# A masked softmax on one core: fewer control instructions on VectorE, and GpSimd's set-up inside its loop

## The chip, the core and the metric

The kernel runs on one core of a Trainium2 chip. The core has compute engines that run their own instruction streams and meet at semaphores: TensorE (PE), VectorE (DVE), ScalarE (ACT) and GpSimd (POOL); a fifth, SyncE (SP), issues DMAs. Sixteen DMA engines move data between HBM, the chip's main memory, and SBUF, the core's on-chip memory of 128 partitions. The metric is device time in microseconds (us) of one execution, the median of several runs.

## The reference

The input is `x`, float32 of 16 batches x 8 heads x 256 x 256, and `lengths`, 16 integers, one per batch, drawn from 128 to 255. For each batch the first `length` columns of each row get a softmax and the rest is zero:

```python
for b in range(batch):
    length = lengths[b]
    masked = x[b, :, :, :length].copy()
    masked = masked - np.max(masked, axis=-1, keepdims=True)
    exp_masked = np.exp(masked)
    result[b, :, :, :length] = exp_masked / np.sum(exp_masked, axis=-1, keepdims=True)
```

`x` and the result are 33.55 MB each. Columns beyond a batch's length need not be read.

## The kernel before

A batch is one tile of 128 partitions x 16 rows x 256 columns, 2.1 MB. Eight such tiles fit in SBUF (`xt`, 8 slots), and batch b uses slot b mod 8. A batch goes through five steps.

1. Load. SyncE issues the loads of batches 0 to 3 whole, at the start (L130, L132). GpSimd issues those of batches 4 to 15, two to a turn of a loop of six turns (L177). It reads the batch's length into a register (`length`, L120) and goes through a tree of branches (`pick`, L147) to one of twelve DMAs that differ in the width they load: 160 to 240 columns in steps of 8, or all 256. The tree stands twice in the program, for the even and the odd batch of a turn. From the second turn on, each load first waits until the load two batches before it has landed (`s_sw`) and until the store that frees its slot has landed (`s_st`).
2. Clip. VectorE takes the minimum of the tile and a value that is hugely negative beyond the length (`clip`, L218; L221): `down` is -1e30 x (column + 0.5), `len_s` is 1e30 x length. So no length is needed in an address. `mask` (L230) waits for the load and then clips columns 128 to 255, and, under a branch on the length (L238), columns 0 to 127 as well. With the lengths given, the branch is never entered.
3. Exponential. ScalarE runs over half tiles, 32 turns of a loop, with eight activations each that also sum their row (L326). No maximum is subtracted. A half turn i waits for `s_min` of i + 1; a whole clip adds 2, a half clip (batch 0) adds 1.
4. Divide. VectorE takes the reciprocal of eight row sums per partition (L245) and multiplies the half tile (L248).
5. Store. SyncE issues the stores of a batch in one to three parts (L141). Each waits for the divided half; a batch's first one waits also until the store two batches before has landed (L140). The very first store waits until ScalarE has done three halves (L134).

VectorE's order is written out by hand: the clip of the next batch comes after the first divided half of this one (batch 0 and batches 4 on) or ahead of it (batches 1 to 3).

Before its loop, GpSimd runs a set-up: the column numbers (`iota`, L164), constants for two small matmuls (L167, L168), two one-element memsets that stand in for stores that do not exist (L170), and, after VectorE has `len_s`, four memsets that fill columns 160 to 255 of slots 4 to 7 (L173), since a narrow load leaves them unwritten. It then waits for the lengths, the fills and batch 2's load (L176).

At the end a check looks whether any row sum is out of range (L274, L277; a matmul adds the flags over the partitions, L191). If so, all batches are done again with the maximum subtracted, in a slow loop at the end of VectorE's and ScalarE's programs (L293, L336). With the data given, it is not entered.

Of the kernel before, what the change touches and what calls it, by code (L numbers as in the profile page):

```python
# [9 lines left out]
F32 = mybir.dt.float32  # L10
# [11 lines left out]
def kernel(  # L22
# [6 lines left out]
    nc = tc.nc  # L29
# [13 lines left out]
    ahead = 4  # L43
    assert slots - ahead == 4 and batch % slots == 0

# [35 lines left out]
    ones_c = pool.tile([P, 1], BF16, name="ones_c")  # L81
    ends = pool.tile([P, 2], F32, name="ends")
    bad = pool.tile([P, 2], BF16, name="bad")
    count = psum.tile([1, 2], F32, name="count")
    redo = pool.tile([1, 1], F32, name="redo")
# [7 lines left out]
    with tc.tile_critical(no_gpsimd_drain=True):  # L93
# [53 lines left out]
        def pick(v, n, slot, par, ws):  # L147
# [15 lines left out]
        o_g = out_f.rearrange("b p t c -> p b (t c)")  # L163
        nc.gpsimd.iota(  # L164
            iota_i, pattern=[[1, seq_k]], base=0, channel_multiplier=0
        ).then_inc(s_iota, 1)
        nc.gpsimd.memset(ones, 1.0).then_inc(s_ones, 1)  # L167
        nc.gpsimd.memset(ones_c, 1.0).then_inc(s_ones, 1)  # L168
        for par in range(2):
            nc.gpsimd.memset(seed[:, par : par + 1], 0.0).then_inc(s_st[par], 64)  # L170
        nc.gpsimd.wait_ge(s_v, 2)
        for b in range(ahead, slots):
            nc.gpsimd.memset(xt[:, b, :, low:], 0.0).then_inc(s_fill, 1)  # L173
        nc.gpsimd.wait_ge(s_word, 16)
        nc.gpsimd.wait_ge(s_fill, slots - ahead)
        nc.gpsimd.wait_ge(s_ld[ahead - 1], 16)  # L176
        with nc.Fori(0, (batch - ahead) // 2, 1, engines=[POOL]) as q:  # L177
            for par in range(2):
                n = 2 * q + (ahead + par)
                v_len = length(POOL, word[0:1, bass.ds(2 * n, 1)])  # L180
                with nc.gpsimd.If(q >= 1):  # L181
                    nc.gpsimd.wait_ge(s_sw[par], 16 * q)
                    nc.gpsimd.wait_ge(s_st[par], 64 * q)
                pick(v_len, bass.ds(n, 1), bass.ds(n % slots, 1), par, widths + [seq_k])

# [3 lines left out]
        nc.tensor.matmul(len_f, lhsT=ones, rhs=len_b, start=True, stop=True).then_inc(s_lenf, 1)  # L189
        nc.tensor.wait_ge(s_bad, 2)  # L190
        nc.tensor.matmul(count, lhsT=ones_c, rhs=bad, start=True, stop=True).then_inc(s_count, 1)  # L191
# [4 lines left out]
        def step(ins):  # L196
            nonlocal v
            v += 1
            ins.then_inc(s_v, 1)
# [30 lines left out]
        def mask(b, s):  # L230
            v_len = length(DVE, word[0:1, 2 * b : 2 * b + 1])
            if b == 0:
                nc.vector.wait_ge(s_ld[s.start // half], 16)
            elif b < ahead:
                nc.vector.wait_ge(s_ld[b + 1], 16)
            else:
                nc.vector.wait_ge(s_sw[b % 2], 16 * ((b - ahead) // 2 + 1))
            with nc.vector.If(v_len < mid):  # L238
                clip(b, s, 0, mid)
            clip(b, s, mid, seq_k).then_inc(s_min, (s.stop - s.start) // half)  # L240

# [28 lines left out]


        sums = row_sum.rearrange("p b t -> p (b t)")
        for k, op in enumerate((ALU.max, ALU.min)):
            step(nc.vector.tensor_reduce(out=ends[:, k : k + 1], in_=sums, op=op, axis=AX))  # L274
        nc.vector.wait_ge(s_v, v)
        for k, (edge, op) in enumerate(((sum_high, ALU.is_gt), (sum_low, ALU.is_lt))):
            nc.vector.tensor_scalar(  # L277
                out=bad[:, k : k + 1],
                in0=ends[:, k : k + 1],
                scalar1=edge,  # L280
                scalar2=None,
                op0=op,
            ).then_inc(s_bad, 1)
# [8 lines left out]
        with nc.vector.Else():  # L292
            with nc.Fori(0, batch, 1, engines=[DVE]) as i:  # L293
# [12 lines left out]
                ).then_inc(g_v, 1)  # L306
                nc.vector.wait_ge(g_exp, i + 1)
                nc.vector.reciprocal(out=inv_g, in_=sum_g).then_inc(g_v, 1)
# [11 lines left out]
        sum_h = row_sum.rearrange("p b (h j) -> p (b h) j", h=2)  # L320
        with nc.Fori(0, 2 * batch, 1, engines=[ACT]) as i:
            nc.scalar.wait_ge(s_min, i + 1)
            at = bass.ds(i % (2 * slots), 1)
            for j in range(half):
                e = x_h[:, at, j, :]
                ins = nc.scalar.activation(  # L326
                    out=e, in_=e, func=EXP, accum_out=sum_h[:, bass.ds(i, 1), j]
                )
            ins.then_inc(s_exp, 1)

        nc.scalar.wait_ge(s_redo, 1)
        a_redo = length(ACT, redo_bits[0:1, 0:1])
        with nc.scalar.If(a_redo >= 1):
            for par in range(2):
                nc.scalar.wait_ge(s_st[par], 64 * (batch // 2 + 1))
            with nc.Fori(0, batch, 1, engines=[ACT]) as i:  # L336
                nc.scalar.dma_start(out=g_t, in_=x_g[:, bass.ds(i, 1)]).then_inc(g_ld, 16)
                nc.scalar.wait_ge(g_v, 3 * i + 2)
                for t in range(nt):
                    ins = nc.scalar.activation(  # L340
                        out=g_t[:, t],
                        in_=g_t[:, t],
                        func=EXP,
                        bias=neg_max[:, t : t + 1],
                        accum_out=sum_g[:, t : t + 1],
                    )
                ins.then_inc(g_exp, 1)
                nc.scalar.wait_ge(g_out, i + 1)
# [37 lines left out]
```

## Time and profile before

| what | us |
|---|---|
| median of 3 runs | 156.16 (155.8 to 156.35) |
| the profiled execution's own time | 156.34 |
| its span, first to last instruction of the kernel | 154.7 |
| DVE busy | 116.6 (75%) |
| ACT busy | 105.2 (68%) |
| POOL busy | 19.0 (12%) |
| last load landed | 134.2 |
| last store issued | 147.1 |

Times within the profile count from the span's start. Busy time of an engine leaves out its branches, register operations and waits. A queue's share is the time of its packets over sixteen DMA engines' span. A name such as DVEq is an engine's sequencer, which handles the instructions that are not counted as busy. In the chain of waits each step is followed back to what released it, and "issue" is time for which the trace shows no reason.

### The profile page before, as it was taken

The page shows a single profiled execution, that of the slowest core. Times are in us where ns is not written, and L with a number is a line of the kernel's source. Part 1 is how long each engine was busy: PE and PEld are TensorE (multiplying, and loading weights), DVE is VectorE, ACT ScalarE, POOL GpSimd, SP SyncE. Part 2 cuts the span into 40 slices and gives each one's busy share as a digit, 9 for nine tenths or more (in the row PEclk, how much of TensorE's full clock was granted, in tenths as well). Part 3 has the DMA queues.
Part 4 walks back from the last instruction along what each step waited for, and adds up shares of the span by engine and source line. Part 5 has one row for each costly group of instructions (what it writes and reads, how often), then busy time and mean ns, then how long its engine had stood idle before and what let it go on. Part 6 is the DMA issues. An engine that isn't in the chain of part 4 may idle for free.

```text
span 154.7 us, 1341 instructions
## 1 busy us (share of the span) xinstructions
PE 0.3 (0%) x2; PEld 0.2 (0%) x2; DVE 116.6 (75%) x89; ACT 105.2 (68%) x514; POOL 19.0 (12%) x26
## 2 busy tenths in 40 slices
PE   0000000000000000000000000000000000000000
PEld 0000000000000000000000000000000000000000
DVE  1349999953999696979879696969669619696820
ACT  3097799992692959688695959595964914959300
POOL 4910031000220200202020020202001000000000
DMA  3999999999999999999999999999999999999991
GB/s 114 430 447 419 441 373 420 403 407 447 406 403 391 410 410 417 412 416 412 404 422 409 415 412 409 421 414 412 415 424 415 416 437 432 422 447 424 424 426 76
DMA packets 9989, 62.09 MB, mean 401 GB/s; under 512 B 850, under 2 KB 946, under 8 KB 6274
## 3 DMA queue, kind: packets, MB, share of 16 engines
q1 hardware_dynamic: 5904, 41.95, 65.7%
q0 software_dynamic: 4080, 20.12, 32.1%
q14 instruction: 3, 0.02, 0.0%
q10 hardware_dynamic: 2, 0.00, 0.0%
HBM read 28.51 MB, written 33.55 MB: 401 GB/s over the span
## 4 chain that ended last, share of the span: by engine, by line
DMA 77%; issue 7%; DVE 4%; ACT 3%; POOLq 3%; SPq 1%; ACTq 0%; POOL 0%; PE 0%; DVEq 0%
DMA xt<-in_x_dram 77%; ACT xt L326 3%; DVE xt L221 2%; DVE xt L248 1%; POOLq L120 1%; POOLq L156 1%; POOLq L151 1%; SPq L130 1%; DVE ends L274 0%; ACTq L326 0%; POOL xt L151 0%; SPq L132 0%; POOLq L181 0%; DVE bad L277 0%; DVE inv_sum L245 0%
## 5 line engine op out<-in xcount | busy, mean ns | idle before, releaser
L326 ACT ACTIVATE xt<-xt x256 | 102.4, 402 | 37.7 <-DVE xt L221 37.7
L248 DVE TENSOR_TENSOR xt<-xt,inv_sum 128x2048 f32<-128x2048 f32 x32 | 73.3, 2291 | 1.1
L326 ACT ACTIVATION_READ_ACCUMULATOR xt<-xt x256 | 48.0, 188 | 0.0
L221 DVE SCALAR_TENSOR_TENSOR xt<-down,len_s,xt 128x2048 f32<-128x2048 f32 (+1 forms) x17 | 37.8, 2221 | 13.6 <-DMA xt<-in_x_dram 13.5
L151 POOL DMA_DIRECT2D xt<-in_x_dram x12 | 12.8, 1064 | 96.0 <-DMA out_dram<-xt 54.2
L245 DVE RECIPROCAL inv_sum<-row_sum 128x8 f32<-128x8 f32 x32 | 6.3, 198 | 14.4 <-ACT xt L326 14.4
L173 POOL MEMSET xt<- 128x1536 f32 x4 | 5.3, 1391 | 1.1 <-DVE len_s L212 1.1
L318 ACT ACT_TABLE_LOAD x1 | 1.3, 1283 | 1.6 <-SPq L93 1.6
L204 DVE TENSOR_SCALAR down<-iota_i 128x256 f32<-128x256 int32 x1 | 0.3, 301 | 1.6 <-POOL iota_i L164 1.6
L274 DVE TENSOR_REDUCE ends<-row_sum 128x1 f32<-128x256 f32 x2 | 0.7, 411 | 0.0
L191 PE MATMUL count<-bad,ones_c 128*1 128x2 bf16 x1 | 0.2, 164 | 145.3 <-DVE bad L277 145.3
L209 DVE CAST len_b<-word 1x16 bf16<-1x16 int32 x1 | 0.2, 164 | 0.4 <-DMA word<-in_lengths_dram 0.4
L212 DVE TENSOR_SCALAR len_s<-len_f 128x16 f32<-128x16 f32 x1 | 0.2, 173 | 0.3 <-PE len_f L189 0.3
L164 POOL IOTA iota_i<- 128x256 int32 x1 | 0.3, 331 | 0.6 <-SPq L93 0.6
L285 DVE TENSOR_REDUCE redo<-count 1x1 f32<-1x2 f32 x1 | 0.1, 148 | 0.3 <-PE count L191 0.3
L191 PEld LDWEIGHTS count<-bad,ones_c 128*1 128x1 bf16 x1 | 0.1, 79 | 145.4 <-DVE bad L277 145.4
L170 POOL MEMSET seed<- 1x1 f32 x2 | 0.2, 226 | 0.0
L277 DVE TENSOR_SCALAR bad<-ends 128x1 bf16<-128x1 f32 x2 | 0.2, 152 | 0.0
L318 ACT ACTIVATE warm<-const-float32-0.0 128x1 f32<-128x1 f32 x1 | 0.2, 204 | 0.0
L167 POOL MEMSET ones<- 1x128 bf16 x1 | 0.2, 196 | 0.0
L189 PE MATMUL len_f<-len_b,ones 1*128 1x16 bf16 x1 | 0.2, 165 | 2.6 <-DVE len_b L209 2.6
L370 POOL MEMSET const-float32-0.0<- 128x1 f32 x1 | 0.1, 98 | 0.3 <-issue 0.3
(6 smaller groups left out, 0.5 us busy)
## 6 DMA issues: line engine op xcount, KB each, us to landing
out_dram<-xt SPq DMA_DIRECT2D x19, 1024.0 KB
out_dram<-xt SPq DMA_DIRECT2D x14, 512.0 KB
xt<-in_x_dram SPq DMA_DIRECT2D x3, 2048.0 KB, 16.0
out_dram<-xt SPq DMA_DIRECT2D x3, 2048.0 KB
xt<-in_x_dram POOLq DMA_DIRECT2D x3, 1728.0 KB, 16.9
xt<-in_x_dram POOLq DMA_DIRECT2D x2, 2048.0 KB, 18.5
xt<-in_x_dram POOLq DMA_DIRECT2D x2, 1600.0 KB, 17.1
xt<-in_x_dram POOLq DMA_DIRECT2D x2, 1280.0 KB, 15.1
```

What stands on the lines that cost most here:

```text
L120: return nc.values_load(at, engines=[engine], skip_runtime_bounds_check_because="compared with constants, never an address",)
L130: nc.sync.dma_start(out=xt[:, 0, s], in_=x_f[0, :, s]).then_inc(s_ld[h], 16)
L151: nc.gpsimd.dma_start(out=xt[:, slot, :, :w], in_=x_n[:, n, :, :w]).then_inc(s_sw[par], 16)
L156: with nc.gpsimd.If(v <= ws[m]):
L173: nc.gpsimd.memset(xt[:, b, :, low:], 0.0).then_inc(s_fill, 1)
L191: nc.tensor.matmul(count, lhsT=ones_c, rhs=bad, start=True, stop=True).then_inc(s_count, 1)
L221: return nc.vector.scalar_tensor_tensor(out=t, in0=down[:, None, lo:hi].to_broadcast([P, s.stop - s.start, hi - lo]), scalar=len_s[:, b : ...
L245: step(nc.vector.reciprocal(out=inv_sum[:, b, s], in_=row_sum[:, b, s]))
L248: nc.vector.tensor_tensor(out=t, in0=t, in1=inv_sum[:, b, s, None].to_broadcast([P, half, seq_k]), op=ALU.mult,).then_inc(s_out, 1)
L274: step(nc.vector.tensor_reduce(out=ends[:, k : k + 1], in_=sums, op=op, axis=AX))
L318: nc.scalar.activation(out=warm, in_=nc.const_aps.tensor(0.0, (P, 1), F32), func=EXP)
L326: ins = nc.scalar.activation(out=e, in_=e, func=EXP, accum_out=sum_h[:, bass.ds(i, 1), j])
```

## The change

VectorE: `mask` no longer reads the length and no longer branches; it clips columns 128 to 255 alone. In place of the branch, the check at the end gets a third test, whether the smallest length is under 128; if it is, the slow loop redoes all batches. `s_min` now counts one per clip, so ScalarE's half turn i waits for i // 2 + 2. ScalarE's first half turn is written out before the loop, with constant addresses. In the slow loop, sixteen activations in a row become a loop.

GpSimd: the loop gets a turn more. Turn 0 goes to the `Else` of a branch, where the set-up now stands, behind the code of the loads; the turns from 1 on run the loads with q = (turn + 7) mod 8, which is turn - 1.

```diff
-    ends = pool.tile([P, 2], F32, name="ends")
-    bad = pool.tile([P, 2], BF16, name="bad")
-    count = psum.tile([1, 2], F32, name="count")
+    ends = pool.tile([P, 3], F32, name="ends")
+    bad = pool.tile([P, 3], BF16, name="bad")
+    count = psum.tile([1, 3], F32, name="count")
...
-        nc.gpsimd.iota(
-            iota_i, pattern=[[1, seq_k]], base=0, channel_multiplier=0
-        ).then_inc(s_iota, 1)
...
-        with nc.Fori(0, (batch - ahead) // 2, 1, engines=[POOL]) as q:
-            for par in range(2):
-                n = 2 * q + (ahead + par)
-                v_len = length(POOL, word[0:1, bass.ds(2 * n, 1)])
-                with nc.gpsimd.If(q >= 1):
-                    nc.gpsimd.wait_ge(s_sw[par], 16 * q)
-                    nc.gpsimd.wait_ge(s_st[par], 64 * q)
-                pick(v_len, bass.ds(n, 1), bass.ds(n % slots, 1), par, widths + [seq_k])
+        turns = (batch - ahead) // 2
+        with nc.Fori(0, turns + 1, 1, engines=[POOL]) as turn:
+            with nc.gpsimd.If(turn >= 1):
+                q = nc.s_assert_within(
+                    (turn + 7) % 8, 0, turns - 1, skip_runtime_bounds_check_because="turn >= 1"
+                )
+                for par in range(2):
+                    n = 2 * q + (ahead + par)
+                    v_len = length(POOL, word[0:1, bass.ds(2 * n, 1)])
+                    with nc.gpsimd.If(turn >= 2):
+                        nc.gpsimd.wait_ge(s_sw[par], 16 * q)
+                        nc.gpsimd.wait_ge(s_st[par], 64 * q)
+                    pick(v_len, bass.ds(n, 1), bass.ds(n % slots, 1), par, widths + [seq_k])
+            with nc.gpsimd.Else():
+                nc.gpsimd.iota(
+                    iota_i, pattern=[[1, seq_k]], base=0, channel_multiplier=0
+                ).then_inc(s_iota, 1)
...
+                nc.gpsimd.wait_ge(s_ld[ahead - 1], 16)
...
-        nc.tensor.wait_ge(s_bad, 2)
+        nc.tensor.wait_ge(s_bad, 3)
...
         def mask(b, s):
-            v_len = length(DVE, word[0:1, 2 * b : 2 * b + 1])
...
-            with nc.vector.If(v_len < mid):
-                clip(b, s, 0, mid)
-            clip(b, s, mid, seq_k).then_inc(s_min, (s.stop - s.start) // half)
+            clip(b, s, mid, seq_k).then_inc(s_min, 1)
...
-        for k, op in enumerate((ALU.max, ALU.min)):
-            step(nc.vector.tensor_reduce(out=ends[:, k : k + 1], in_=sums, op=op, axis=AX))
+        checks = (
+            (sums, ALU.max, sum_high, ALU.is_gt),
+            (sums, ALU.min, sum_low, ALU.is_lt),
+            (len_s, ALU.min, mid * big, ALU.is_lt),
+        )
+        for k, (values, op, _, _) in enumerate(checks):
+            step(nc.vector.tensor_reduce(out=ends[:, k : k + 1], in_=values, op=op, axis=AX))
...
-        with nc.Fori(0, 2 * batch, 1, engines=[ACT]) as i:
-            nc.scalar.wait_ge(s_min, i + 1)
-            at = bass.ds(i % (2 * slots), 1)
+        def rows(at, i):
...
+        nc.scalar.wait_ge(s_min, 1)
+        rows(slice(0, 1), slice(0, 1))
+        with nc.Fori(1, 2 * batch, 1, engines=[ACT]) as i:
+            nc.scalar.wait_ge(s_min, i // 2 + 2)
+            rows(bass.ds(i % (2 * slots), 1), bass.ds(i, 1))
```

## The prediction

> **What bounds the kernel now.** I read the page's slices and queues first, then a table by stage, then the chain that ended last, then single lines.
>
> ```profile
> span 154.7 us, 1341 instructions
> DMA  3999999999999999999999999999999999999991
> GB/s 114 430 447 419 441 373 420 403 407 447 406 403 391 410 410 417 412 416 412 404 422 409 415 412 409 421 414 412 415 424 415 416 437 432 422 447 424 424 426 76
> q1 hardware_dynamic: 5904, 41.95, 65.7%
> q0 software_dynamic: 4080, 20.12, 32.1%
> q14 instruction: 3, 0.02, 0.0%
> HBM read 28.51 MB, written 33.55 MB: 401 GB/s over the span
> ```
>
> The DMA row is 9 in 38 of 40 slices, and the two data queues (q1: SyncE's four loads and all stores; q0: GpSimd's loads) fill 97.8% of sixteen engines. The change moves the same 62.09 MB. Could compute still matter in one stage? The table by stage (length; busy PE, PEld, DVE, ACT, POOL; clock; DMA share; GB/s) says no:
>
> ```profile
> 2.50:20.00 17.50, 0.17 (x1) 0.10 (x1) 11.18 (x9) 10.65 (x52) 5.33 (x4) 1.00 1.00 421
> 20.00:26.00 6.00, 0.00 (x0) 0.00 (x0) 5.93 (x6) 6.00 (x32) 1.85 (x2) 1.00 0.99 389
> 44.00:126.00 82.00, 0.00 (x0) 0.00 (x0) 67.67 (x48) 61.06 (x302) 9.75 (x9) 1.00 1.02 413
> 134.20:150.20 16.00, 0.16 (x1) 0.08 (x1) 12.02 (x13) 8.47 (x42) 0.00 (x0) 1.00 1.01 428
> 150.20:154.70 4.50, 0.00 (x0) 0.00 (x0) 0.00 (x0) 0.00 (x0) 0.00 (x0) 1.00 0.32 135
> ```
>
> Their share is 0.99 to 1.02 (packets overlap a little) from 2.5 to 150.2 us, even in the stage after the last load. What is left is the last line: the sixteen engines do not finish together. In the semaphore events of the trace, the last store (half of batch 15) lands on its sixteen engines from 151.50 to 153.49 us: median 151.8, the two latest 152.94 and 153.49. SyncE waits for the latest, so the end belongs to the most loaded DMA engine.
>
> The chain of waits seems to contradict this near its end:
>
> ```profile
> 116.60 17.58 DMA xt<-in_x_dram
> 134.21 0.06 DVEq L238
> 134.26 1.20 issue
> 135.47 2.35 DVE xt L221
> ```
>
> It shows a branch (L238) and then 1.20 us of "issue" before the last clip. That is not the branch's price: VectorE's multiply (L248) started at 133.26 and takes 2.29 us, so VectorE was simply busy until 135.5.
>
> **The change, part by part.** The profiled run took 156.34 us: its span of 154.72 and 1.62 around it, which nothing here touches. The median of the runs is 156.16, 0.18 less.
>
> *VectorE's length reads and branches go.* They are 17 register loads and 17 branches:
>
> ```profile
> L120 DVEq TENSOR_LOAD <-word x17: 311/751/1532, 3.0 to 133.3; - x17
>   DMA xt<-in_x_dram: 13.5, 5
> ```
>
> 17 loads at a median of 0.75 are 12.8 us, but each follows a multiply of 2.29 us in the engine's queue and runs beside it. If that cover went, up to 1.5 us would show per batch. The branch shows only where VectorE waits for a load (5 times, second line, which is of the clip L221): for batch 4 the branch is at 37.30 and the clip at 37.51, so 0.2 us each and 1.0 in all. None of it reaches the end, because the DMA engines have other packets: I take 0. Early in the run it makes the clip of batch 0 start 0.2 earlier, and with ScalarE's first half written outside its loop (a register operation of 0.11 and one of 0.05 between the wait at 7.83 and the activation at 8.07) the first store, which waits for ScalarE's third half and leaves at 19.80, goes about 0.2 us earlier. It then shares the engines with loads that would have had them: 0, at most 0.2 gained.
>
> *ScalarE's wait value.* One shift more in 31 turns, by the ALU_OP rows 0.035 to 0.05 us. ScalarE waits 37.7 us for VectorE, so it hides, except after the last clip, where it delays the last store by 0.05. The cover there: batch 15's first half lands at 149.06 to 151.04 and its second 2.44 later on every engine, so the second was queued in time. It was issued at 147.14; SyncE's first load took 1.04 from issue (1.13) to first packet (2.17); the first engine was free at about 148.6. So 0.4 us of delay is free, and 0.05 costs 0.
>
> *The end check.* One reduction (between the 0.15 of L285 and the 0.41 of L274) and one comparison (0.15) more on VectorE after its last multiply. All engines but SyncE are through by 149.9, SyncE by 153.5: 0, with 3.4 us of cover. The changes in the redo branch do not run.
>
> *GpSimd's set-up moves behind the loop's code.* It issues one iota (0.33), four small memsets (0.6 in all) and four fills (1.39 each), and three waits; no DMA. Before it come a loop start and a branch, 0.2 to 0.5 us by the L177 and L181 rows, and perhaps the fetch of a distant piece of code, about 1.7 us if it takes what passes from the backward branch at 24.01 to the end of the fetch at 25.72. VectorE, behind the iota, sits idle for 3.53 us before its first clip; the fills end at 8.38 and are needed at 18.54. Both cover it: 0. Set-up later than 3.4 us would move the clip.
>
> *Each turn of GpSimd's loop* gets a branch and two register operations, some 0.3 us. In turns after the first they stand before waits that last 4 to 12 us. The first two loads have no such cover: the turn starts with the backward jump (0.26 by 24.01 to 24.28), so the first goes at about 21.3 instead of 20.77. SyncE's queue covers that: by 26.4, when q0's first packet runs, it has issued 12.6 MB (four loads, batch 0's store and all of batch 1's) and the engines have moved 9.9 (by the table 0.1, 7.4 and 2.3, and 0.1 after it), so 2.7 MB or some 6 us of work are still queued. 0, up to that.
>
> *The instruction fetches.* Three packets of 8192 bytes ran in the span: at 25.41, 60.66 and 151.27 us, each 0.309 us on one DMA engine. After the first, the next packet took 0.695 instead of 0.611, so a fetch costs its engine 0.31 to 0.39. The first comes 1.4 us after GpSimd's first backward jump; after the change GpSimd visits the end of its code at about 1 us, before the engines are full, so this fetch should move there, for nothing. The second falls amid VectorE's program, which loses some 50 instructions; it goes, or comes later at the same price. What are they worth? Nothing, if their engines are not the latest ones (lower end 0); 0.78 if both sit on the latest one and no other takes over. The latest engine's lead in landing over the next was 0.05 at batch 3's load (23.74, 23.79), 0.45 at batch 0's store (29.62, 30.07), 0.47 at batch 7's load (61.25, 61.72) against 0.21 at batch 6's (51.67, 51.88): it grew by 0.40 and 0.26 across the two fetches. That speaks for the upper end. It is cut off at 0.55, where the next engine (152.94) sets the end. I take 0.55.
>
> Sum: 156.34 - 0.55 = 155.79 for the profiled run, 155.6 for the median.
>
> The Trainium skill, page "Runtime: NRT & Kernel Launch", section "Instruction fetch mechanics", speaks against the change: code is prefetched in sequence only, and a taken branch out of the resident window stalls for a fetch. The trace bears it out in part: GpSimd's loop jumped back five times, and the queue of instructions shows no packet at those times but for the first.
>
> **The rivals.**
>
> *A: no difference* (156.1). The fetches sit on engines that have slack, or come again later in the run. For it: they are 0.02 MB of 62, and the packets carry no engine's name. Against it: the two steps in the lead.
>
> *B: slower by code that is fetched again.* The first turn now runs the last piece of GpSimd's code, and then jumps back over all of it. Where that piece has displaced the loop's first one, each of the six loading turns brings at least one fetch: 6 x 0.39 = 2.3 us on one DMA engine, less the 0.55 gained: 157.9. It decides from the second such fetch on (0.78 against 0.55). Against it: the loop of before, with the same two trees of twelve loads, stayed resident. By the skill's rule above it would go this way.
>
> *C: slower by the mix.* In pure reads or writes the engines run at 428 to 431 GB/s, in the mixed stage at 413, and at 389 where stores set in (20 to 26 us). If the earlier store and the later loads bring another stretch like that, 6 x (1 - 389/421) = 0.5 us, and one more like the slices of 403 and 391 (3.87 x (10 + 22)/413 = 0.3 us), it ends at 156.9 with the fetches still there. For it: which packets meet is set by just such shifts. Against it: the shifts are 0.2 and 0.5 us long.
>
> **How the numbers follow.** Chances: forecast 0.42, A 0.30, B 0.14, C 0.14. About 0.3%, 0.47 us, is what a measurement can tell here from no change (the three runs span 155.8 to 156.35). The forecast, with a range of its own from 155.0 to 155.7 (a gain from the bound of 0.47 to the 1.2 that the fourth-latest engine, 152.25, allows), counts as faster, A as the same, B and C as slower. The range goes from 154.9, just past that engine, to 157.5 (B with five fetches, 5 x 0.39 - 0.55 = 1.4); a tenth is left out on each side.
>
> **What would show it.** Right: the instruction queue's packets at 25 and 60 us gone or within the first 3 us; the last landings closer together than 1.99 us; the DMA row still 9 throughout; L120 without VectorE; the first GpSimd load near 21.3. Wrong: more than three instruction packets (B); a lower rate in the same stages (C); a landing order as before (A); or a DMA row below 9, which would mean that a wait of GpSimd's or VectorE's reaches the queues.

## The result and the profile after

The changed kernel takes 156.61 us (median of 15 runs, 155.86 to 157.12) beside 156.15 for the kernel before (15 runs, 155.66 to 156.5). The ratio is 1.0027, with a 95% interval from 1.0014 to 1.0039: 0.4 to 0.5 us slower, just inside the 0.3% that the prediction named as the limit of what can be told from no change, and with a sign that is clear. A gain of 0.55 us was forecast.

The page of the profile after (slices, queues and memory traffic):

```profile
span 155.5 us, 1321 instructions
DMA  4999999999999999999999999999999999999992
GB/s 112 428 436 438 421 430 413 367 406 438 387 405 393 407 413 425 405 426 404 403 415 408 423 404 416 416 401 407 424 410 424 414 441 426 419 451 405 390 428 95
q1 hardware_dynamic: 5904, 41.95, 65.5%
q0 software_dynamic: 4080, 20.12, 32.2%
q14 instruction: 3, 0.02, 0.0%
HBM read 28.51 MB, written 33.55 MB: 399 GB/s over the span
```

The same bytes, the same number of packets, still three instruction packets, and engines that are still full: two data queues at 97.7%. The span is 0.8 us longer. The profiled execution took 157.12 us, the slowest of the 15 runs and 0.51 above their median; the one of before (156.34) was 0.19 above its own. So the traces differ by 0.78 us, and the medians by 0.46. What follows from the trace of the changed kernel holds for that one execution.

The table by stage of the kernel after (length; busy time of PE, PEld, DVE, ACT, POOL; clock; DMA share; GB/s):

```profile
2.50:20.00 17.50, 0.17 (x1) 0.10 (x1) 10.83 (x11) 10.17 (x49) 5.38 (x6) 1.00 0.99 417
20.00:26.00 6.00, 0.00 (x0) 0.00 (x0) 5.93 (x5) 6.00 (x31) 1.85 (x2) 1.00 1.02 426
26.00:44.00 18.00, 0.00 (x0) 0.00 (x0) 13.56 (x11) 13.69 (x69) 1.16 (x1) 1.00 1.00 401
44.00:126.00 82.00, 0.00 (x0) 0.00 (x0) 68.26 (x48) 61.46 (x304) 9.76 (x9) 1.00 1.02 412
140.00:144.00 4.00, 0.00 (x0) 0.00 (x0) 2.81 (x3) 4.00 (x21) 0.00 (x0) 1.00 0.92 389
```

Two of these rows of the kernel before were not shown yet:

```profile
26.00:44.00 18.00, 0.00 (x0) 0.00 (x0) 13.48 (x10) 13.62 (x69) 1.16 (x1) 1.00 1.00 416
140.00:144.00 4.00, 0.00 (x0) 0.00 (x0) 2.74 (x3) 4.00 (x22) 0.00 (x0) 1.00 1.03 438
```

The mix of loads and stores is hardly the place. The slow stretch of before at 20 to 26 us (389) is gone (426), but 26 to 44 us fell from 416 to 401. Together, 6 x 389 + 18 x 416 is 9.82 MB before and 6 x 426 + 18 x 401 is 9.77 MB after: 0.05 MB or 0.1 us. From 2.5 to 20 us (417 for 421) and over the long middle (412 for 413) some 0.07 and 0.08 MB are lost, 0.2 us each, but a rate is rounded by as much in the middle. The largest single loss is at 140 to 144 us: 389 for 438, or 0.20 MB, and a share of 0.92, so 0.3 us in which the engines had nothing to do. All batches are loaded by then, and the stores that are left wait for compute.

What comes later at the start? Single lines of the timeline of the kernel after (start, length, engine and line, idle time before and what ended it):

```profile
7.04 1.28 DVE L228 SCALAR_TENSOR_TENSOR xt<-down,len_s,xt 128x1024 f32<-128x1024 f32 x1 [3.94 <-DMA xt<-in_x_dram]
...
20.28 0.42 SPq L141 DMA_DIRECT2D out_dram<-xt  x1
...
22.12 1.29 POOL L151 DMA_DIRECT2D xt<-in_x_dram  x1 [13.63 <-issue]
```

and the same of the kernel before:

```profile
6.51 1.28 DVE L221 SCALAR_TENSOR_TENSOR xt<-down,len_s,xt 128x1024 f32<-128x1024 f32 x1 [3.53 <-DMA xt<-in_x_dram]
...
19.80 0.42 SPq L141 DMA_DIRECT2D out_dram<-xt  x1
...
20.77 1.29 POOL L151 DMA_DIRECT2D xt<-in_x_dram  x1 [12.39 <-issue]
```

In both, the first clip is released by the load and not by GpSimd's `iota`, so the set-up, which came 0.6 us later (the `iota` at 1.84 instead of 1.24), was not what anybody waited for. It is the load itself that is late: the first half of batch 0 has landed on fifteen engines at 6.25 us (before: 6.23) and on the last at 6.93 (before: 6.26). The packet records show most of the reason. An instruction packet ran at 4.71 us, 0.309 us long, on the DMA engine whose share of batches 0 to 3 ends last, and the data packet behind it took 0.521 instead of 0.309. That is 0.31 and 0.21, so 0.52 us of delay; what the other 0.15 us are was not found. Without the 0.52 us this engine would have landed at 6.41, an estimate, and still last. GpSimd itself did not wait for the packet: its set-up ran from 1.75 us on, so the packet did not bring the first code that it went to. Batches 1 and 2 then land at 14.31 and 19.21 on this engine, 0.68 and 0.69 later than before, while the second-latest engine is within 0.02 (13.64 for 13.62, 18.52 for 18.51).

GpSimd waits for batch 2 before its first load. That load went 1.35 us later, which is 0.69 from the landing and 0.66 from its way to the load: 2.89 us from the end of the wait (19.23) to the load, against 2.23 before (18.54 to 20.77).

Why does compute come later at the end? From the chain of waits after:

```profile
107.56 20.80 DMA xt<-in_x_dram
128.39 2.36 DVE xt L228
...
134.56 2.29 DVE xt L252
136.85 2.27 DVE xt L228
```

and from VectorE's timeline before:

```profile
127.08 2.35 DVE L221 SCALAR_TENSOR_TENSOR xt<-down,len_s,xt 128x2048 f32<-128x2048 f32 x1 [3.25 <-DMA xt<-in_x_dram]
```

The load that was waited for is that of batch 14, the last but one. It landed at 126.79 on the second-latest engine and at 128.36 on the latest; before, at 126.58 and 126.85. So it was in time on all engines but one, and on that one 1.5 us later than before. VectorE sat idle until then, and from its clip on (128.39 for 127.08) everything is 1.3 us later: the last clip (136.77 in the timeline, before 135.47) and the last store (issued at 148.46, before 147.14). The last batch's load was late as well (135.72 on the latest engine, before 134.18), but no clip waited for it: VectorE was busy with a multiply until 136.85, as it was until 135.5 before. The stores ran dry meanwhile. The last store landed at 154.26 on the latest engine (153.49) and at 152.82 on the median one (151.81).

VectorE's reads, by the view of the line that reads the lengths (times of one: least, median, most; first and last start), after:

```profile
L120 DVEq TENSOR_LOAD <-redo x1: 1171/1171/1171, 149.9 to 149.9; - x1
```

VectorE's seventeen reads of `word` are gone; the one that is left reads the outcome of the check, as before.

### The profile page after: what moved, and what is told of

Its sections match the earlier page's. It is cut to its first block, busy times and chain, and to the rows that moved or that the text cites. A ratio compares the mean times of both kernels' runs of the same rounds, so it can differ in the third digit from the quotient of the medians.

```text
span 155.5 us, 1321 instructions
## 1 busy us (share of the span) xinstructions
PE 0.3 (0%) x2; PEld 0.2 (0%) x2; DVE 116.9 (75%) x91; ACT 105.2 (68%) x514; POOL 19.0 (12%) x26
## 2 busy tenths in 40 slices
DMA packets 9989, 62.09 MB, mean 399 GB/s; under 512 B 850, under 2 KB 946, under 8 KB 6274
## 4 chain that ended last, share of the span: by engine, by line
DMA 66%; DVE 16%; ACT 5%; issue 5%; SPq 2%; ACTq 1%; POOLq 1%; PE 0%
DMA xt<-in_x_dram 34%; DMA out_dram<-xt 31%; DVE xt L252 9%; DVE xt L228 6%; ACT xt L335 5%; ACTq L335 1%; SPq L141 1%; DVE inv_sum L249 1%; SPq L130 1%; DVE ends L284 0%; POOLq L120 0%; SPq L132 0%; POOLq L156 0%; POOLq L151 0%; DVE bad L287 0%
## 5 line engine op out<-in xcount | busy, mean ns | idle before, releaser
L335 ACT ACTIVATE xt<-xt (+1 forms) x256 | 102.4, 402 | 39.0 <-DVE xt L228 39.0
L335 ACT ACTIVATION_READ_ACCUMULATOR xt<-xt (+1 forms) x256 | 47.9, 187 | 0.0
```

The lines of the kernel that those rows point to most:

```text
L335: ins = nc.scalar.activation(out=e, in_=e, func=EXP, accum_out=sum_h[:, i, j])
```

## The experiments

Three theories. **T1**: the instruction fetch that follows GpSimd's visit to the end of its code falls into the load of batch 0, on the DMA engine that is last anyway, and this delay goes through to the end. **T2**: what costs is that VectorE's chain begins later (first clip 7.04 for 6.51), for whatever reason. **T3**: VectorE's and ScalarE's part of the change moves the traffic into a worse mix. All ratios are to the kernel before, run beside on the same chip.

### Each half of the change alone

*GpSimd's half* (`pool_part`), with VectorE's and ScalarE's programs as before:

```diff
-        nc.gpsimd.iota(
-            iota_i, pattern=[[1, seq_k]], base=0, channel_multiplier=0
-        ).then_inc(s_iota, 1)
...
-        with nc.Fori(0, (batch - ahead) // 2, 1, engines=[POOL]) as q:
+        turns = (batch - ahead) // 2
+        with nc.Fori(0, turns + 1, 1, engines=[POOL]) as turn:
+            with nc.gpsimd.If(turn >= 1):
...
+            with nc.gpsimd.Else():
+                nc.gpsimd.iota(
```

> The kernel before with GpSimd's part of the change alone (set-up as turn 0 of the loop, behind the loads' code). Theory 1, the early fetch: the changed kernel's profile has the instruction packet of 25.4 us at 4.7 us, where it holds up one DMA engine by 0.52 us (0.309 and a next packet of 0.521 instead of 0.309) in the middle of batch 0's load; GpSimd's part carries the whole loss: ratio 1.002 to 1.005, a fetch before 6 us, the first half of batch 0 complete at about 6.9 us instead of 6.26. Theory 2, the late start: the same time, because VectorE's chain starts 0.5 us later. Theory 3, the order of VectorE and ScalarE: GpSimd's part costs nothing, 0.999 to 1.001.

Measured: 156.92 us (156.85 to 156.97), 1.0044 [1.0030, 1.0058]. The fetch at 4.77 us, batch 0's first half at 6.25 and 6.98, the first clip at 7.24. Rows of its table by stage:

```profile
20.00:26.00 6.00, 0.00 (x0) 0.00 (x0) 5.93 (x5) 6.00 (x32) 1.85 (x2) 1.00 1.02 429
26.00:44.00 18.00, 0.00 (x0) 0.00 (x0) 13.81 (x11) 13.95 (x71) 1.16 (x1) 1.00 1.00 401
...
140.00:144.00 4.00, 0.00 (x0) 0.00 (x0) 2.50 (x2) 4.00 (x21) 0.00 (x0) 1.00 1.00 426
```

The loss is in this half. And it does not need the dry stretch at 140 us: here the engines are full there (1.00), and the last store still lands 0.54 us later than before on the latest engine (154.03 for 153.49), 0.23 on the median one (152.04 for 151.81). These are single executions; by all runs the half costs 0.44%, or 0.69 us (0.47 to 0.91). Compute is not late in this kernel: its last store was issued at 146.89, before at 147.14. So its end is later by work that the DMA engines still had to do, and not by a wait for compute. The same holds for `early_visit` and `after_few` below (146.73 and 146.41).

*VectorE's and ScalarE's half* (`vector_part`), with GpSimd as before:

```diff
-            v_len = length(DVE, word[0:1, 2 * b : 2 * b + 1])
...
-            with nc.vector.If(v_len < mid):
-                clip(b, s, 0, mid)
-            clip(b, s, mid, seq_k).then_inc(s_min, (s.stop - s.start) // half)
+            clip(b, s, mid, seq_k).then_inc(s_min, 1)
...
+                nc.scalar.wait_ge(s_min, i // 2 + 2)
```

> The kernel before with VectorE's and ScalarE's part alone (no length reads, no branches, first half turn written out, third check); GpSimd as before. Theories 1 and 2: no loss, 0.998 to 1.000, the instruction packet near 25 us again, first clip at about 6.35 us (0.15 earlier than before). Theory 3: this part carries the loss, 1.002 to 1.005, with lower GB/s in the mixed stage.

Measured: 156.12 us (155.84 to 156.59, 12 runs), 0.9998 [0.9985, 1.0011]. So this half costs nothing and gains nothing, and T3 falls. In the execution that was profiled, all of the loads happened to come late (batch 0's first half at 7.00 on the latest engine, 6.48 on the median one), as its first clip shows:

```profile
7.11 1.28 DVE L222 SCALAR_TENSOR_TENSOR xt<-down,len_s,xt 128x1024 f32<-128x1024 f32 x1 [4.12 <-DMA xt<-in_x_dram]
```

VectorE's chain began as late as in the changed kernel, and this execution took 155.99 us, among the fastest. That speaks against T2, with one execution. It also shows that a late start of the loads need not reach the end. Two rows of its table by stage:

```profile
2.50:20.00 17.50, 0.16 (x1) 0.10 (x1) 10.73 (x9) 10.15 (x49) 5.33 (x4) 1.00 0.95 403
20.00:26.00 6.00, 0.00 (x0) 0.00 (x0) 5.93 (x5) 6.00 (x31) 1.85 (x2) 1.00 1.01 430
```

Up to 20 us it is 0.32 MB behind the kernel before (403 for 421), and from 20 to 26 us it regains 0.25 of them (430 for 389).

### Is it VectorE's later start, or GpSimd's?

*The first clip held back* (`delay_clip`): the kernel before, with a reduction between the first landing and the first clip.

```diff
+        nc.vector.wait_ge(s_ld[0], 16)
+        nc.vector.tensor_reduce(out=idle_out, in_=down, op=ALU.max, axis=AX)
```

> The kernel before with one more reduction of 256 columns (0.41 us) on VectorE between batch 0's first landing and its clip, so that the chain behind it starts 0.4 to 0.45 us later with no fetch moved. Theory 2: this alone gives the loss, 1.002 to 1.004. Theory 1 and 3: 0.999 to 1.001, since the DMA engines' queues cover it.

Measured: 156.24 us, 1.0017 [0.9995, 1.0038]. The first clip went at 7.28 instead of 6.51, the first store at 20.54. The runs scatter too widely (155.89 to 157.62) to rule out either theory; the medians differ by 0.06 us.

*A later set-up* (`late_setup`): the kernel before with a memset of 640 columns ahead of the `iota`.

```diff
+        nc.gpsimd.memset(idle_out, 0.0)
         nc.gpsimd.iota(
```

> The kernel before with one more memset of 640 columns (about 0.6 us) ahead of GpSimd's iota: the set-up late by the same 0.6 us as in the changed kernel, no visit, no moved fetch. Theory 1: 0.999 to 1.001. Rival, the late set-up: 1.003 to 1.005.

Measured: 156.14 us, 1.0003 [0.9993, 1.0013]; the first clip at 6.53. A late set-up is free, as the prediction had it.

*A later first load* (`late_loads`): the kernel before with a memset of 1.4 us between GpSimd's last wait and its loop.

```diff
+        nc.gpsimd.memset(idle_out, 0.0)
         with nc.Fori(0, (batch - ahead) // 2, 1, engines=[POOL]) as q:
```

> The kernel before with one more memset of 1.39 us on GpSimd between its last wait (18.5 us) and its first load, so that the first load goes at about 22.1 us as in the changed kernel, with the code, the loop and the fetch at 25 us as before. Theory 1, the early fetch: 0.999 to 1.001. Rival, the late first loads: 1.002 to 1.004.

Measured: 156.22 us, 1.0008 [0.9995, 1.0020], but the load was not late. GpSimd's timeline:

```profile
18.55 1.38 POOL L178 MEMSET idle_out<- 128x1536 f32 x1 [10.17 <-DMA xt<-in_x_dram]
20.68 1.29 POOL L152 DMA_DIRECT2D xt<-in_x_dram  x1 [0.75 <-issue]
```

The memset ran beside the register operations and branches of the loop's start, and the load went at 20.68 (before: 20.77). So this run says nothing on late loads.

### The fetch moved in time

The next kernels enter turn 0 at other times, or with less in it, so that GpSimd's visit to the end of its code, and the fetch, fall elsewhere.

*Visit after batch 0* (`late_visit`): the whole change, but with the set-up ahead of the loop and only the three waits in turn 0, which is entered when batch 0 has landed.

```diff
+        nc.gpsimd.wait_ge(s_ld[1], 16)
         turns = (batch - ahead) // 2
...
             with nc.gpsimd.Else():
-                nc.gpsimd.iota(
...
                 nc.gpsimd.wait_ge(s_word, 16)
```

> The changed kernel, but the set-up stands ahead of the loop again, and turn 0 holds only the three last waits and is entered after batch 0 has landed (8.7 us). So GpSimd still visits the end of its code early, but its fetch falls into batch 1 to 3's loads, between 9 and 16 us. Theory 1: batch 0 lands at 6.3 us again and the engine is held up later, where batch 1's clip has 0.1 to 0.3 us of slack: 0.999 to 1.002. Theory 2: VectorE's chain starts as before, 0.999 to 1.001. Theory 3: the loss of the changed kernel remains, 1.002 to 1.005.

*Visit with the fills* (`early_visit`): VectorE and ScalarE as before; `iota` and the small memsets ahead of the loop, the fills and the waits in turn 0.

```diff
+            with nc.gpsimd.Else():
+                nc.gpsimd.wait_ge(s_v, 2)
+                for b in range(ahead, slots):
+                    nc.gpsimd.memset(xt[:, b, :, low:], 0.0).then_inc(s_fill, 1)
+                nc.gpsimd.wait_ge(s_word, 16)
```

> GpSimd's loop as in the changed kernel, VectorE and ScalarE as before; but the small part of the set-up (iota, ones, seeds) stands ahead of the loop, and turn 0 holds only the fills and the waits. So VectorE's constants come as early as before, while GpSimd still goes to the end of its code at about 2 us. Theory 1, the early fetch: instruction packet between 4 and 6.3 us, batch 0's first half 0.4 to 0.7 us late on one DMA engine, ratio 1.003 to 1.006 as with GpSimd's part whole (1.0044). Rival, the late set-up: no loss, 0.999 to 1.001.

*Visit last* (`last_visit`): VectorE and ScalarE as before; set-up and waits ahead of the loop, and in turn 0 a single wait that is long over.

```diff
         nc.gpsimd.wait_ge(s_ld[ahead - 1], 16)
-        with nc.Fori(0, (batch - ahead) // 2, 1, engines=[POOL]) as q:
+        with nc.Fori(0, turns + 1, 1, engines=[POOL]) as turn:
...
+            with nc.gpsimd.Else():
+                nc.gpsimd.wait_ge(s_word, 16)
```

> The same loop, but the whole set-up and its waits stand ahead of it, and turn 0 holds one wait that is long over. So GpSimd visits the end of its code when batch 2 has landed (18.5 us), the fetch comes at 20 to 25 us as before the change, and what is left of GpSimd's part is the longer way to the first load (22.1 us instead of 20.8). Theory 1: no loss, 0.999 to 1.0015. Rival, the later loads: 1.003 or more.

*The branch's arms swapped* (`setup_first`, the whole change; `setup_first_pool`, GpSimd's half alone): the set-up is still turn 0, but stands ahead of the loads' code.

```diff
-            with nc.gpsimd.If(turn >= 1):
+            with nc.gpsimd.If(turn < 1):
+                nc.gpsimd.iota(
...
-            with nc.gpsimd.Else():
-                nc.gpsimd.iota(
+            with nc.gpsimd.Else():
+                q = nc.s_assert_within(
```

> The changed kernel whole, with the same swap: set-up ahead of the loads' code, still as turn 0. Theory 1: packet at 20 us or later, 0.998 to 1.001. Rival, the loop: 1.002 to 1.004 as the changed kernel.

> GpSimd's part alone, with the same loop of seven turns and the same branch, but the set-up ahead of the loads' code in the program instead of behind it. GpSimd then runs turn 0 without going to the end of its code. Theory 1, the early fetch: the packet of 4.7 us moves back to 20 us or later, batch 0's first half lands at 6.3 us, and the loss of GpSimd's part (1.0044 with the set-up behind) goes: 0.999 to 1.0015. Rival, the loop and the late first loads: 1.003 or more.

*Fewer widths* (`after_few`, `before_few`, `vector_few`): seven widths instead of twelve, those that the given lengths use, so the same bytes move; tried on the changed kernel, the kernel before and VectorE's half, to make GpSimd's code shorter.

```diff
-    widths = list(range(160, 248, 8))
+    widths = [160, 168, 184, 200, 216, 224]
```

> The changed kernel with seven widths (160, 168, 184, 200, 216, 224, 256) instead of twelve in GpSimd's two trees: these are the ones that the given lengths use, so every load has the same bytes, and GpSimd's code is shorter by ten loads. Theory 1, the early fetch: if the end of the code now lies in what is loaded already, there is no instruction packet before 6.3 us, batch 0's first half lands at 6.3 us on all engines, and the loss is gone: 0.997 to 1.001. If a packet is still there at 4 to 6 us, the loss stays: 1.002 to 1.005. A rival by which GpSimd's loop itself (its branches and register operations) costs the time: 1.002 to 1.005 also without the packet.

> The kernel before with the seven widths. It prices a fetch in the middle of the run: if the packet of 25.4 us is gone, the prediction's term said 0.39 us gained where its engine is the last one (0.9975); rival A of the prediction said nothing (0.999 to 1.001).

> VectorE's and ScalarE's part with the seven widths, GpSimd's set-up ahead of the loop. With the fetch at 25 us gone and that of VectorE's program at 74 us instead of 60: 0.996 to 0.998 by the prediction's term, 0.999 to 1.001 by rival A. If it is clearly under 1 it is the version that beats both.

What the runs gave. The fetch is that of GpSimd's code, by the packet records; landings are from the semaphore events, on the latest of the sixteen engines; all but the ratio are of one profiled execution. An execution's time is 2.85 or 2.86 us more than its latest landing in every row, so that column tells no more than the time of this one execution, and the runs of one kernel lie up to 1.5 us apart; the ratio is of all runs.

| kernel | GpSimd's fetch | batch 0, first half | first GpSimd load | last store landed: median, latest | ratio [95%] |
|---|---|---|---|---|---|
| before | 25.41 | 6.26 | 20.77 | 151.81, 153.49 | 1 |
| late_setup | 25.36 | 6.27 | 20.81 | 152.04, 153.41 | 1.0003 [0.9993, 1.0013] |
| vector_part | 25.49 | 7.00 | 21.49 | 152.16, 153.13 | 0.9998 [0.9985, 1.0011] |
| after | 4.71 | 6.93 | 22.12 | 152.82, 154.26 | 1.0027 [1.0014, 1.0039] |
| pool_part | 4.77 | 6.98 | 22.16 | 152.04, 154.03 | 1.0044 [1.0030, 1.0058] |
| early_visit | 6.03 | 6.55 | 22.20 | 152.19, 153.91 | 1.0033 [1.0016, 1.0049] |
| after_few | 4.61 | 6.81 | 22.01 | 152.01, 153.80 | 1.0013 [0.9998, 1.0027] |
| late_visit | 13.41 | 6.44 | 22.27 | 152.37, 153.52 | 1.0008 [0.9991, 1.0025] |
| last_visit | 23.28 | 6.36 | 25.09 | 152.53, 153.16 | 1.0013 [0.9997, 1.0029] |
| setup_first_pool | 23.17 | 6.24 | 24.97 | 152.43, 153.17 | 1.0011 [0.9996, 1.0026] |
| setup_first | 23.80 | 6.45 | 25.61 | 153.41, 153.72 | 1.0024 [1.0011, 1.0037] |

The other two with seven widths gave 1.0004 [0.9993, 1.0016] (`before_few`) and 1.0000 [0.9984, 1.0016] (`vector_few`). Fewer widths did not take the fetch away: it ran at 4.61 us in `after_few` and at 27.66 and 26.89 in the other two. So `after_few` tests nothing that `after` does not, and is a fourth kernel of its kind.

What follows. First, the fetch goes where GpSimd's visit goes: it ran at 4.6 to 6.0 us where turn 0 is entered early, at 13.4 us where it is entered after batch 0, and at 23 to 28 us in all others. Second, three of the four kernels with the fetch at 4.6 to 6.0 us are clearly slower than the kernel before, and so is only one of the others in the table, `setup_first`. Third, `pool_part` and `setup_first_pool` are the closest pair: the same loop and the same turns, and only the place of the set-up in the code differs. With the set-up behind the loads' code the loss is 0.44%, with it ahead 0.11%, and the intervals do not overlap, though GpSimd's first load is 2.8 us later in the second. So neither the longer loop nor a late first load makes the loss of `pool_part` by itself. That is T1's side.

T1 is not proven by this. `late_visit`, with the first load as late as in `after` (22.27), was slower by 0.08%, but its interval overlaps that of `after`; `after_few` (1.0013) is not to be told from `last_visit` (1.0013). The batch 3 of `late_visit` lands at 25.36 on the latest engine, even later than in `after` (24.97; before 23.79), so a late engine at 24 us does not reach the end by the same amount. In `pool_part` itself the latest engine is 0.73 us behind the next at batch 0 (6.98, 6.25), 1.85 at batch 5 (44.80, 42.95) and 0.03 at batch 15 (133.90, 133.87): there the lag does not last through the loads. And T1 expected `setup_first` to lose nothing, but it lost as much as the change.

`setup_first` lost it in another way. Its first GpSimd load in the timeline, and its last stage:

```profile
25.61 1.29 POOL L151 DMA_DIRECT2D xt<-in_x_dram  x1 [17.23 <-issue]
```

```profile
140.00:144.00 4.00, 0.00 (x0) 0.00 (x0) 2.81 (x3) 4.00 (x20) 0.00 (x0) 1.00 0.80 340
```

GpSimd's program stopped at 21.33, in the middle of its first load, and went on at 25.58: 4.26 us where the kernel before takes 0.68 (20.07 to 20.75). Between them, at 23.80, ran the fetch. The data queue did not run dry at the start, but batch 14, for which the clip waits, landed at 128.98 (before 126.85), the last store was issued at 149.08 (147.14), the share fell to 0.80 at 140 to 144 us, and there the end lost what it had in hand. The sixteen engines then finish together, at 153.34 to 153.72: the end is now set by a wait for compute that all of them share and no longer by the most loaded engine. `last_visit`, with VectorE's program as before, shows the same stop, somewhat shorter (its first load at 25.09, its share at 140 to 144 us 0.92), and the price is not clear of nothing (1.0013).

So where the set-up stands decides when the code of this loop is fetched. With the set-up behind the loads' code, the branch to it is taken at 1.2 us, the fetch follows at 4.7, and GpSimd's next instruction is 0.5 us behind the branch; with the set-up ahead of it, the fetch comes at 23 to 24 us, in the middle of the first load, and GpSimd stops. The kernel before does neither: its fetch ran at 25.41, behind its first two loads (20.77 and 23.96), while its next load was not due before 38.65.

### What does an early packet cost?

*One packet* (`extra_packet`): the kernel before, with a load of 8188 bytes that ScalarE issues behind the lengths, on one DMA engine.

```diff
+        nc.scalar.dma_start(
+            out=extra, in_=x_f[1, 0:1].rearrange("p t k -> p (t k)")[:, 0:2047]
+        ).then_inc(s_extra, 16)
```

> The kernel before with one more load of 8188 bytes into one partition, issued by ScalarE right behind the lengths: one packet of about 0.31 us on one DMA engine at 2 to 3 us, beside the fetch at 25 us. Theory 1 in the form that any delay of one engine at the start reaches the end: 1.002 to 1.005. Theory 1 in the form that only the engine that is last anyway counts: 0.999 to 1.001, unless the packet happens to lie on that engine.

Measured: 156.04 us, 0.9998 [0.9985, 1.0011]. The packet ran at 5.12 us and took 0.309 us, on an engine whose share of batches 0 and 1 ends at 12.74 us where the latest ends at 13.21. Batch 0's first half still landed at 6.24. A packet of a fetch's size at a fetch's time is free on an engine that has slack.

*A packet on every engine* (`extra_all`), *the same in the middle* (`extra_all_mid`, issued by SyncE behind batch 0's store; landed at 30.4 to 31.5 us) *and on eight engines* (`extra_eight`): each packet is 16384 bytes.

```diff
+        nc.scalar.dma_start(out=extra[:: P // 16], in_=x_f[1, 0:16]).then_inc(s_extra, 16)
```

```diff
             if b == 0:
+                nc.sync.dma_start(out=extra[:: P // 16], in_=x_f[1, 0:16]).then_inc(s_extra, 16)
```

```diff
+        nc.scalar.dma_start(out=extra[:: P // 8], in_=x_f[1, 0:8]).then_inc(s_extra, 16)
```

> The kernel before with one more load of 16 x 16384 bytes, one packet of 0.61 us on each of the sixteen DMA engines, issued by ScalarE right behind the lengths, so that it falls into batch 0's load. As bytes alone it costs 0.61 us (ratio 1.004). If delay of the early loads costs more than its bytes (theory 1 in the form: what is lost before the pipeline has filled is lost again behind it), 1.006 or more, and clearly over the same packets at 20 to 25 us.

> The same 16 packets of 16384 bytes, but issued by SyncE behind batch 0's store, so that they run at 20 to 25 us. As bytes alone 0.61 us, ratio 1.004. If only early delay counts, less than the early ones: 1.000 to 1.003.

> Eight such packets, on eight of the sixteen engines, early as in the first. If the end belongs to the engine that is last anyway: 1.004 or more when it is among the eight (then the first landings show a latest engine 0.6 us later than 6.26), and 0.999 to 1.001 when it is not (latest landing 6.3 to 6.6, second-latest group moved instead).

Measured: `extra_all` 157.74 us, 1.0095 [1.0073, 1.0117]; `extra_all_mid` 157.55, 1.0085 [1.0063, 1.0108]; `extra_eight` 157.99, 1.0111 [1.0087, 1.0135]. At the rate of before (62.09 MB in about 151 us) the bytes of the first two are worth 0.64 us, those of the third 0.32; they cost 1.46, 1.27 and 1.71. So this work on the engines is paid in full and more, early as in the middle of the run, and half the bytes on half the engines cost no less than all of them on all. The expectations of `extra_all_mid` and `extra_eight` both missed. In `extra_eight` the first half of batch 0 landed at 6.27, as before, which by its expectation meant no cost; the packets ran from 5.7 to 8.6 us and met the second half instead. The table by stage of `extra_eight`, for the time of the packets:

```profile
4.00:10.00 6.00, 0.00 (x0) 0.00 (x0) 1.28 (x1) 1.91 (x9) 4.41 (x4) 1.00 1.04 340
```

The share stays above 1 and the rate falls to 340 (363 in `extra_all`), where `extra_packet` has 433: the engines are busy, with packets that took up to 1.55 us. The second half of batch 0 landed at 11.03 in `extra_eight` (8.74 before). In these runs the delay of the first 10 us was not made up later; in the execution of `vector_part` shown above most of a delay of 0.7 us was. They are heavier than one fetch, and don't price it.

## Why the prediction was wrong

*What sets the end.* Right: the DMA engines are full in both kernels, and the end is the landing of the last store on the latest of them (153.49, 154.26).

*VectorE's reads and branches.* Right at 0: without them the time is 0.9998 of before. Even the 0.2 us for the first batch are there: from batch 0's landing to the first store 13.35 us pass (6.93 to 20.28), before 13.54 (6.26 to 19.80). But the landing moved by 0.67, so the first store came later and not earlier. ScalarE's shift and the end check showed nowhere, as forecast; they were in `vector_part` too.

*GpSimd's set-up.* It came 0.6 us later, where 0.2 to 0.5 was said, and was covered by VectorE's idle time, as said: the first clip waits for the load.

*The first GpSimd load.* 21.3 was forecast and 22.12 came. The step counted the extra turn (0.53; it took 0.66) and not that batch 2, for which GpSimd waits, would land 0.69 later. The cover named there held: q0's first packet came at 27.53, and the DMA share stayed at 1.02 and 1.00. With the load at 25.1 and 25.0 (`last_visit`, `setup_first_pool`) the kernels lost 0.13% and 0.11%, with intervals that include no loss; at 25.6 with VectorE's half (`setup_first`), 0.24%.

*The instruction fetches.* This step failed, and the 0.55 us with it. It said that GpSimd "visits the end of its code at about 1 us, before the engines are full, so this fetch should move there, for nothing". The visit was at 1.2 us (the branch at 1.225). The packet ran at 4.71, 2.5 us after the first data packets (2.16 us), in the middle of batch 0's load, on the latest engine, and cost it 0.52 us, not 0.31 to 0.39. So nothing was saved: an engine paid early instead of at 25 us, and more. In place of the 0.55 us gained, GpSimd's half alone lost 0.69 (0.47 to 0.91). What had been looked at was when the fetch is asked for, and what counts is when its packet gets its turn. The second fetch was hedged ("goes, or comes later at the same price"): it came later. It runs at 74.5 to 77.0 us in all six kernels with VectorE's half, and at 58.7 to 61.7 in the kernels without. `vector_part` shows that moving it gains nothing. No run was without a fetch, so the term's size, the price of a fetch in the middle of the run, stays untested.

*The lead of the latest engine.* The forecast took 0.40 and 0.26 us of growth across the two fetches as their price at the end, cut off at the second-latest engine. A late engine at 24 us does not stay late by the same amount: in `late_visit` batch 3 came 1.57 us later than before on the latest engine, and the kernel lost 0.08% (at most 0.25%, 0.4 us). Already in the trace before, the lead also shrank between the two fetches, from 0.44 at batch 4 (36.83, 37.27) to 0.21 at batch 5 (43.16, 43.37). So its growth across a fetch is no measure of what the fetch costs at the end.

*The rivals.* A (no difference, 156.1) was nearest: the fetches come again at other times, and the loss of 0.27% lies inside its bound, though with a clear sign. That 156.61 lies in the range of 154.9 to 157.5 says nothing for the forecast, which went the other way. B (code fetched again in each turn) did not happen: three instruction packets, as before. The rule of the Trainium skill, "Runtime: NRT & Kernel Launch", section "Instruction fetch mechanics", that a taken branch out of the resident code stalls for a fetch, fits where the code is not there yet: `setup_first` stopped for 4.26 us, with the fetch in that time. At the later backward jumps no stall for a fetch shows, in before and after alike; the rule speaks of targets outside the resident code, and no run shows which those are, so this does not go against it. The packets here have 8192 bytes where this section of the Trainium skill speaks of blocks of 16 KiB. C (a worse mix) did not happen over 20 to 44 us (9.82 and 9.77 MB). Its sign named in advance, a lower rate in the same stages, is there from 26 to 44 us, and is nearly taken back by the stage ahead of it.

*What stays open.* That GpSimd's half makes the loss is shown. So is, for that half alone, that the place of the set-up behind the loads' code makes most of it (0.44% against 0.11% with it ahead), and not the longer loop or the late first load. That this works through the early fetch is the reading that fits best: 0.52 us held up on the latest engine, and no clear loss in three of the four kernels where the added turn's fetch comes later. It is not shown, because no run has the set-up there without the fetch, and how the delay of one engine gets through 150 us to the end was not followed; in `pool_part` no engine lags at the last load. The fourth of those kernels, `setup_first`, lost by a stop of GpSimd instead. In the one profiled execution of the changed kernel, the dry stretch at 140 to 144 us adds to the loss; `pool_part` has none (1.00), and how much of the 0.46 us it makes was not separated. None of the versions is clearly faster than the kernel before: the best are VectorE's half (0.9998) and the same with seven widths (1.0000).

## What to carry to other kernels

Where all DMA engines are full from the first microseconds, a code fetch is not free because its branch is taken early: here its packet ran 2.5 us after the first data, on the latest engine, and the load that everything waits for was late. On an engine with slack a packet of that size cost nothing. Before placing code so that it is fetched early, look at where the fetch's packet will run, and whether the fetch at its old place had a wait of its engine over it; here GpSimd had one of nearly 12 us (25.5 to 37.3). Branches and register reads beside a full multiply or a wait for a load were worth nothing, 17 of each.

## What was not expected of the hardware

- A fetch whose branch was taken at 1.2 us ran at 4.7 us, and the data packet behind it took 0.521 instead of 0.309 us, alike (0.520 and 0.521) in `pool_part` and `after_few`; in `early_visit`, with the branch at 1.4 us, the fetch ran at 6.0 and the next packet took 0.522. An ordinary 8188-byte load at 5.12 us moved no landing.
- GpSimd stopped for 3.6 to 4.3 us, with its fetch in that time, while the engines were full (from 21.2–21.5 to 25.0–25.6 in `last_visit`, `setup_first_pool`, `setup_first`), although the packet itself takes 0.31 us and was over by 24.1 at the latest.
- Eight packets of 16 KB on eight engines cost 1.71 us, sixteen on sixteen 1.46: more than twice what the bytes are worth. The added packets took up to 1.55 us each meanwhile, where one of 16 KB elsewhere takes 0.61.
